# The last sum of a decoder layer: VectorE's adds for twelve of sixteen tiles become TensorE identity products

## Chip, cores, metric

The kernel runs on one core of a Trainium2 chip. The metric is device time in microseconds (us) of one execution, as the median of several. Lower is better.

## What is computed

One step of a decoder layer for 288 tokens (256 of a prompt, 32 samples) and a model width of 2048. Only the end of it matters here:

```python
hf = rms_norm(x, prm['norm_ffn_pre'][l])
f = jnp.square(jax.nn.relu(hf @ prm['ffn_w1'][l])) @ prm['ffn_w2'][l]
x = x + rms_norm(f, prm['norm_ffn_post'][l])

def rms_norm(x, g):
    y = xf * lax.rsqrt(jnp.mean(xf * xf, axis=-1, keepdims=True) + RMS_EPS)
    return (y * g).astype(x.dtype)
```

The last line is the output `o_y`: x plus the FFN output, scaled by one factor per feature (`g`) and one factor per token (the root).

## The kernel before

Activations lie with features on the 128 partitions and tokens along the free axis: x is `x_t`, 16 tiles of 128x288 (float32), in the memory named `arx`. The FFN output is `facc`, 16 tiles in `arm`. All big products run on TensorE as three single-pass products per weight tile (lines 429 to 431), for 1419 of the 1437 us. ScalarE and VectorE split the weights for them meanwhile (lines 393, 394).

The FFN runs in four blocks. In the last, the evacuation of each output tile m (lines 1830 to 1836) adds it into `facc`, squares it on ScalarE into `ssa` or `sqt`, multiplies `facc` by the feature's gain, and adds the squares into `ssa`. What follows the last product is a serial tail that no product covers:

- `sum_cols` (lines 409, 412): TensorE sums the squares over the partitions, first of `ssa`, then of `sqt[1]`, the last tile's squares.
- Square root on ScalarE (line 1848), reciprocal on VectorE (line 1849).
- `spread_cols` (line 418): TensorE spreads the 288 factors over all partitions, into a PSUM tile `ps`.
- For six groups of 1, 3, 4, 4, 3 and 1 tiles (`FIN`): VectorE multiplies `facc` by `ps` (line 1854) and adds it to `x_t` (line 1855); a store of the group follows, on SyncE's and ScalarE's queues in turn (line 1856).

A scheduler sets the order on each engine and adds the waits: every engine has a count that its instructions raise, and an instruction waits until another engine's count has reached a number. Operands are tracked by tile. The PSUM banks that the change uses are slices of one tile, handed out first in, first out:

```python
bt = psb.tile([128, 5, 512], F32, name="bt")
banks = Banks(bt, 5)
```

At the end all five are free.

Of the kernel before, what the change touches and what calls it, by code (L numbers as in the profile page):

```python
# [11 lines left out]
AF = mybir.ActivationFunctionType  # L12
# [5 lines left out]
NT = NP_ + NS  # L18
NB = 8
KT = D // 128  # L20
# [25 lines left out]
LEAD = 4  # L46
PRIO = {"gen_sample_scores": 0, "gen_sample_pv": 0, "gen_prompt_pv": 0.5}
BUDGET = 3.5
FIN = ((0, 1), (1, 3), (4, 4), (8, 4), (12, 3), (15, 1))
BUDO = 3.0  # L50
NSTR, LAG = 2, 3
GATE = 'TQ'
# [259 lines left out]
def build(tc, A, O):  # L312
    nc = tc.nc
    sy, dv, ac, po, pe = nc.sync, nc.vector, nc.scalar, nc.gpsimd, nc.tensor
    with ExitStack() as ctx:
# [12 lines left out]
        rc = cp.tile([128, 12], F32, name="rc")  # L328
        ssa = cp.tile([128, NT], F32, name="ssa")
        sqt = [cp.tile([128, NT], F32, name=f"sqt{i}") for i in range(2)]  # L330
# [6 lines left out]
        ident = ca[:, CA["ident"][0]:][:, :128]  # L337
        ones = ca[:, CA["ones"][0]:][:, :128]
# [9 lines left out]
        banks = Banks(bt, 5)  # L348
# [6 lines left out]
        facc = arm.rearrange("p (k t) -> p k t", k=KT)  # L355
# [48 lines left out]

        TOK = ((0, 0, 128), (1, 128, 128), (2, 160, 128))

        def sum_cols(ps, extra, srcs):

            pe.matmul(out=ps[:, 0:3], lhsT=ident, rhs=extra, start=True, stop=False)
            for j, src in enumerate(srcs):  # L410
                for i, lo, n in TOK:
                    pe.matmul(out=ps[:, i:i + 1], lhsT=src[:, lo:lo + n], rhs=ones[:, 0:1],  # L412
                              start=False, stop=(j == len(srcs) - 1 and i == 2))

        def spread_cols(ps, cols):

            for i, lo, n in ((0, 0, 128), (1, 128, 128), (2, 256, 32)):
                pe.matmul(out=ps[:, lo:lo + n], lhsT=cols[:, i:i + 1].to_broadcast([128, 128]),
                          rhs=ident[:, 128 - n:128], start=True, stop=True)

        def warm(n, lhsT, rhs):

            b = banks.get()
            for _ in range(n):
                pe.matmul(out=b[:, 0:128], lhsT=lhsT, rhs=rhs, start=True, stop=True)  # L425
            banks.put(b)
# [67 lines left out]
        def run_phase(seq, X, evac, budget):  # L494
            ps = None
            for m, h in seq:
                ci = advance()
                if h == 0:
                    ps = psm.tile([128, NT], F32, name="mm", tag="mm")
                for k in range(8):  # L500
                    if k == 6:
                        pump(budget)
                    xh, xl = X(h * 8 + k)
                    mm3(ps, whi[ci][:, k], wlo[ci][:, k], xh, xl, start=(h == 0 and k == 0), stop=(h == 1 and k == 7))
                del whi[ci], wlo[ci]
                st["done"] += 1
                if h == 1:
                    evac(m, ps)

        def tiles(lo, hi):  # L510
            return [(m, h) for m in range(lo, hi) for h in range(2)]
# [6 lines left out]
        x_t = arena.get(KT, NT, order=(0,))  # L518
# [47 lines left out]
        def gen_prenorm():  # L566
            yield 0
            b = banks.get()
            sum_cols(b, rc[:, 9:12], (ssa,))
            ac.activation(out=rc[:, 0:3], in_=b[:, 0:3], func=AF.Sqrt, scale=1.0 / D)  # L570
            dv.reciprocal(out=rc[:, 0:3], in_=rc[:, 0:3])
            spread_cols(b, rc[:, 0:3])
            ac.activation(out=rs_in, in_=b[:, :NT], func=AF.Copy)
            banks.put(b)
            arena.put(sq, x_t)
            S["pre"] = True
            yield 0.5
            sy.dma_start(out=cb, in_=A["c_b"])
            sy.dma_start(out=lora_in, in_=A["lora"][:, 0:512])
            sy.dma_start(out=lora_out, in_=A["lora"][:, 512:1024])  # L580
# [7 lines left out]
        def after(later, earlier):  # L588
            tc.add_manual_dep(later.ins, earlier.ins.name,
                              mybir.DependencyInfo(mybir.DependencyClass.NoSync, mybir.DependencyReason.DATA), reason="order")  # L590
# [1168 lines left out]
        x_t = X2[0]  # L1759
        ensure_split(st["use"] + 3)  # L1760
        ps = psm.tile([128, NT], F32, name="mm", tag="mm")
        sum_cols(ps, rc[:, 9:12], (ssa, sqt[1]))
        for m in range(KT - 2, KT):
            gain(m)
        warm(2, sqt[1][:, 0:128], ident)
        ac.activation(out=rc[:, 0:3], in_=ps[:, 0:3], func=AF.Sqrt, scale=1.0 / D)
        dv.reciprocal(out=rc[:, 0:3], in_=rc[:, 0:3])
        rs = banks.get()
        spread_cols(rs, rc[:, 0:3])
        warm(8, rc[:, 0:1].to_broadcast([128, 128]), ident)  # L1770

# [26 lines left out]
        def gen_ffnorm():  # L1798
            for _ in range(12):
                yield 0  # L1800
            for k in range(KT):
                sq = sqt[k % 2] if k else ssa
                ac.activation(out=sq, in_=x_t[:, k], func=AF.Square)
                if k:
                    dv.tensor_tensor(out=ssa, in0=ssa, in1=sq, op=ALU.add)
                if k % 2:
                    yield 0
            b, = yield from bk(1)
            sum_cols(b, rc[:, 9:12], (ssa,))
            dv.tensor_scalar(out=rc[:, 3:6], in0=b[:, 0:3], scalar1=1.0 / D, scalar2=None, op0=ALU.mult)  # L1810
            banks.put(b)
            yield 0.5
            dv.tensor_scalar(out=rc[:, 6:9], in0=rc[:, 3:6], scalar1=float(D * RMS_EPS), scalar2=None, op0=ALU.mult)
            dv.tensor_tensor(out=rc[:, 6:9], in0=rc[:, 6:9], in1=rc[:, 3:6], op=ALU.mult)
# [10 lines left out]
        def ev_w2(j):  # L1825
            def ev(m, ps):
                if j == 0:
                    ac.activation(out=facc[:, m], in_=ps, func=AF.Copy)
                else:
                    dv.tensor_tensor(out=facc[:, m], in0=ps, in1=facc[:, m], op=ALU.add)  # L1830
                if j == NBLK - 1:
                    sq = sqt[m % 2] if m else ssa
                    ac.activation(out=sq, in_=facc[:, m], func=AF.Square)
                    ac.activation(out=facc[:, m], in_=facc[:, m], func=AF.Copy, scale=pvc("fpost", m))
                    if 0 < m < 15:
                        dv.tensor_tensor(out=ssa, in0=ssa, in1=sq, op=ALU.add)
            return ev

        for j in range(NBLK):
# [3 lines left out]
            assert not gens  # L1843
            run_phase(tiles(0, 16), lambda k: (F["h"][:, k], F["l"][:, k]), ev_w2(j), 3.0)

        ps = psm.tile([128, NT], F32, name="mm", tag="mm")
        sum_cols(ps, rc[:, 6:9], (ssa, sqt[1]))
        ac.activation(out=rc[:, 0:3], in_=ps[:, 0:3], func=AF.Sqrt, scale=1.0 / D)
        dv.reciprocal(out=rc[:, 0:3], in_=rc[:, 0:3])
        ps = psm.tile([128, NT], F32, name="mm", tag="mm")  # L1850
        spread_cols(ps, rc[:, 0:3])
        for q, (lo, n) in enumerate(FIN):
            sl = slice(lo, lo + n)
            dv.tensor_tensor(out=facc[:, sl], in0=facc[:, sl], in1=ps.unsqueeze(1).to_broadcast([128, n, NT]), op=ALU.mult)  # L1854
            dv.tensor_tensor(out=x_t[:, sl], in0=x_t[:, sl], in1=facc[:, sl], op=ALU.add)  # L1855
            (ac if q % 2 else sy).dma_start(out=O["o_y"][:, sl], in_=x_t[:, sl])


def make(arrays):
    import concourse.bacc as bacc  # L1860

    nc = bacc.Bacc("TRN2", target_bir_lowering=False, num_devices=1)
    A = {n: nc.dram_tensor("in_" + n, a.shape, mybir.dt.from_np(a.dtype), kind="ExternalInput").ap() for n, a in arrays.items()}
    O = {n: nc.dram_tensor(n, s, F32, kind="ExternalOutput").ap() for n, s in OUTS.items()}
    with tile.TileContext(nc) as tc:
        build(tc, A, O)
    return nc
# [9 lines left out]
```

## Time and profile before

| | us |
|---|---|
| median of 3 runs | 1439.78 (1439.17 to 1441.64) |
| the profiled execution, its own time | 1438.48 |
| its span in the profile | 1436.7 |
| last big product ends | 1419.4 |
| VectorE's first multiply of the tail starts | 1422.65 |
| VectorE's last add ends | 1433.1 |

In a profile row, PE is TensorE's products, PEld its weight loads, DVE is VectorE, ACT is ScalarE, SPq the queue of SyncE. A float32 product stands as two records (x2), one of the big ones as one. A row gives start, duration, engine, line, operation, out<-in, shape, and in brackets how long the engine idled before it and what ended that.

### The profile page before, as it was taken

The page shows a single profiled execution, that of the slowest core. Times are in us where ns is not written, and L with a number is a line of the kernel's source. Part 1 is how long each engine was busy: PE and PEld are TensorE (multiplying, and loading weights), DVE is VectorE, ACT ScalarE, POOL GpSimd, SP SyncE. Part 2 cuts the span into 40 slices and gives each one's busy share as a digit, 9 for nine tenths or more (in the row PEclk, how much of TensorE's full clock was granted, in tenths as well). Part 3 has the DMA queues.
Part 4 walks back from the last instruction along what each step waited for, and adds up shares of the span by engine and source line. Part 5 has one row for each costly group of instructions (what it writes and reads, how often), then busy time and mean ns, then how long its engine had stood idle before and what let it go on. Part 6 is the DMA issues. An engine that isn't in the chain of part 4 may idle for free.

```text
span 1436.7 us, 27941 instructions
## 1 busy us (share of the span) xinstructions
PE 1399.8 (97%) x11730; PEld 1335.7 (93%) x11730; DVE 834.6 (58%) x1411; ACT 595.5 (41%) x857; POOL 57.4 (4%) x127
## 2 busy tenths in 40 slices
PE   8999999899999999999999999999999999999995
PEld 8899777787878999999999999999999999999995
DVE  7797557445797756794433455544455444555555
ACT  7433323332353534664433344333444333444442
POOL 2101012010101000000000000000000000000000
PEclk9999999999999999999999999999999999999998
DMA  8646678676859964354445444444444444444441
GB/s 291 178 150 213 222 270 265 234 283 219 283 182 379 320 219 163 117 160 165 162 165 172 164 162 165 171 163 164 169 166 163 164 171 164 162 166 169 165 164 79
DMA packets 86190, 276.62 MB, mean 193 GB/s; under 512 B 22400, under 2 KB 26032, under 8 KB 84016
## 3 DMA queue, kind: packets, MB, share of 16 engines
q1 hardware_dynamic: 75280, 212.23, 43.3%
q0 software_dynamic: 9920, 60.83, 11.7%
q8 instruction: 92, 1.51, 0.4%
q10 hardware_dynamic: 864, 1.77, 0.4%
q14 instruction: 34, 0.28, 0.1%
HBM read 267.97 MB, written 6.84 MB: 191 GB/s over the span
## 4 chain that ended last, share of the span: by engine, by line
PE 73%; DVE 1%; DMA 1%; ACT 1%; issue 0%; DVEq 0%
PE mm L429 23%; PE mm L430 23%; PE mm L431 23%; PE bt L1521 1%; DMA arx<-in_vc 1%; DVE arm L1854 0%; DVE arx L1855 0%; PE bt L1146 0%; PE bt L425 0%; ACT ring_h L393 0%; PE bt L1115 0%; DVE ring_l L394 0%; PE mm L412 0%; PE bt L429 0%; PE bt L1165 0%
## 5 line engine op out<-in xcount | busy, mean ns | idle before, releaser
L394 DVE TENSOR_TENSOR ring_l<-w,ring_h 128x1024 fp32r<-128x1024 f32 (+1 forms) x382 | 465.0, 1218 | 388.2 <-ACT ring_h L393 381.2
L393 ACT ACTIVATE ring_h<-w 128x1024 fp32r<-128x1024 f32 (+1 forms) x382 | 402.7, 1055 | 575.0 <-PE mm L430 510.4
L429 PE MATMUL mm<-hh,ring_h 128*128 128x288 f32 x1984 | 597.3, 301 | 5.2 <-ACT ring_h L393 3.3
L430 PE MATMUL mm<-hl,ring_h 128*128 128x288 f32 x1984 | 592.1, 299 | 0.0
L431 PE MATMUL mm<-hh,ring_l 128*128 128x288 f32 x1984 | 589.7, 298 | 0.2 <-DVE ring_l L394 0.2
L429 PEld LDWEIGHTS mm<-hh,ring_h 128*128 128x128 f32 x1984 | 373.4, 188 | 17.0 <-issue 8.5
L431 PEld LDWEIGHTS mm<-hh,ring_l 128*128 128x128 f32 x1984 | 374.6, 189 | 9.2 <-issue 6.3
L430 PEld LDWEIGHTS mm<-hl,ring_h 128*128 128x128 f32 x1984 | 374.3, 189 | 5.6 <-issue 3.3
L430 PE MATMUL mm<-fl,ring_h 128*128 128x288 f32 x1024 | 302.1, 295 | 0.0
L431 PE MATMUL mm<-fh,ring_l 128*128 128x288 f32 x1024 | 301.9, 295 | 0.0
L429 PE MATMUL mm<-fh,ring_h 128*128 128x288 f32 x1024 | 300.3, 293 | 0.0
L429 PEld LDWEIGHTS mm<-fh,ring_h 128*128 128x128 f32 x1024 | 192.5, 188 | 0.0
L430 PEld LDWEIGHTS mm<-fl,ring_h 128*128 128x128 f32 x1024 | 192.5, 188 | 0.0
L431 PEld LDWEIGHTS mm<-fh,ring_l 128*128 128x128 f32 x1024 | 192.4, 188 | 0.0
L1822 ACT ACTIVATE fh<-ft 128x288 fp32r<-128x288 f32 x64 | 28.3, 444 | 78.9 <-DVE ft L1821 78.9
L1830 DVE TENSOR_TENSOR arm<-mm,arm 128x288 f32<-128x288 f32 x48 | 22.0, 458 | 51.0 <-PE mm L431 51.0
L1823 DVE TENSOR_TENSOR fl<-ft,fh 128x288 fp32r<-128x288 f32 x64 | 29.2, 458 | 29.1 <-ACT fh L1822 29.1
L1821 DVE SCALAR_TENSOR_TENSOR ft<-mm,rt 128x288 f32<-128x288 f32 x63 | 28.2, 450 | 0.0
L1820 ACT ACTIVATE rt<-mm 128x288 f32<-128x288 f32 x63 | 24.9, 395 | 0.3 <-PE mm L431 0.3
L1438 PE MATMUL bt<-arm,ar 128*32 128x448 f32 x208 | 23.2, 546 | 1.3 <-DMA arm<-in_kc 1.0
L1729 DVE TENSOR_TENSOR ar<-mm,ar 128x288 f32<-128x288 f32 x32 | 14.5, 454 | 11.4 <-PE mm L431 11.4
L1406 POOL DMA_DIRECT2D arm<-in_kc x26 | 13.7, 528 | 98.3 <-PE bt L1438 90.8
(422 smaller groups left out, 893.1 us busy)
## 6 DMA issues: line engine op xcount, KB each, us to landing
w<-in_w SPq DMA_DIRECT2D x256, 512.0 KB
w<-in_w_in SPq DMA_DIRECT2D x91, 512.0 KB
arm<-in_kc POOLq DMA_DIRECT2D x26, 896.0 KB, 6.9
w<-in_w_out SPq DMA_DIRECT2D x32, 512.0 KB
arm<-in_vc POOLq DMA_DIRECT2D x9, 1024.0 KB, 7.1
ar<-in_vc POOLq DMA_DIRECT2D x7, 1024.0 KB, 7.7
arm<-in_vc POOLq DMA_DIRECT2D x9, 768.0 KB, 8.4
ar<-in_kc POOLq DMA_DIRECT2D x6, 896.0 KB, 7.6
```

The source lines that it names most:

```text
L393: ac.activation(out=h[:, lo:hi], in_=t[:, lo:hi], func=AF.Copy)
L394: dv.tensor_tensor(out=l[:, lo:hi], in0=t[:, lo:hi], in1=h[:, lo:hi].bitcast(F32), op=ALU.subtract)
L429: pe.matmul(out=ps, lhsT=h, rhs=xh, start=start, stop=False)
L430: pe.matmul(out=ps, lhsT=h, rhs=xl, start=False, stop=False)
L431: pe.matmul(out=ps, lhsT=l, rhs=xh, start=False, stop=stop)
L1438: pe.matmul(out=bh[32 * h:32 * h + 32, 0:448], lhsT=qz[:, h, b], rhs=t[:, h], start=(b == 0), stop=(b == NB - 1))
L1729: dv.tensor_tensor(out=macc(m), in0=ps, in1=macc(m), op=ALU.add)
L1820: ac.activation(out=r, in_=ps, func=AF.Relu)
L1821: dv.scalar_tensor_tensor(out=f, in0=ps, scalar=0.0, in1=r, op0=ALU.max, op1=ALU.mult)
L1822: ac.activation(out=fh[:, m], in_=f, func=AF.Copy)
L1823: dv.tensor_tensor(out=fl[:, m], in0=f, in1=fh[:, m].bitcast(F32), op=ALU.subtract)
L1830: dv.tensor_tensor(out=facc[:, m], in0=ps, in1=facc[:, m], op=ALU.add)
```

## The change

Of the sixteen last tiles, twelve (`FIN_PE`) no longer get VectorE's add. For each, TensorE opens a bank with identity times `x_t[:, k]` and, when VectorE has multiplied `facc[:, k]`, closes it with identity times `facc[:, k]`, which accumulates the sum; ScalarE copies the bank into `x_t` and a store takes two tiles. Tiles 12 to 15 stay with VectorE. All stores go through SyncE's queue. Four openings stand ahead of the chain (one inside `sum_cols`, two behind it, one behind `spread_cols`); opening k + 4 stands behind closing k. Multiplies take two tiles each, the last one four.

```diff
-FIN = ((0, 1), (1, 3), (4, 4), (8, 4), (12, 3), (15, 1))
+FIN_PE, FIN_DV = 12, ((12, 2), (14, 2))
...
+        def out_open(k, behind=None):
+            b = banks.get()
+            p = pe.matmul(out=b[:, :NT], lhsT=ident, rhs=x_t[:, k], start=True, stop=False)
+            if behind is not None:
+                after(p, behind)
+            return b
+
         ps = psm.tile([128, NT], F32, name="mm", tag="mm")
-        sum_cols(ps, rc[:, 6:9], (ssa, sqt[1]))
+        sum_cols(ps, rc[:, 6:9], (ssa,), last=False)
+        ob = [out_open(0)]
+        end = sum_cols(ps, None, (sqt[1],))
+        ob += [out_open(1, end), out_open(2, end)]
...
-        spread_cols(ps, rc[:, 0:3])
-        for q, (lo, n) in enumerate(FIN):
+        end = spread_cols(ps, rc[:, 0:3])
+        ob += [out_open(3, end)]
+
+        def times(lo, n):
             sl = slice(lo, lo + n)
             dv.tensor_tensor(out=facc[:, sl], in0=facc[:, sl], in1=ps.unsqueeze(1).to_broadcast([128, n, NT]), op=ALU.mult)
+
+        for lo in range(0, FIN_PE, 2):
+            times(lo, 2)
+            for k in (lo, lo + 1):
+                b = ob[k]
+                end = pe.matmul(out=b[:, :NT], lhsT=ident, rhs=facc[:, k], start=False, stop=True)
+                if k + 4 < FIN_PE:
+                    ob.append(out_open(k + 4, end))
+                ac.activation(out=x_t[:, k], in_=b[:, :NT], func=AF.Copy)
+                banks.put(b)
+            sy.dma_start(out=O["o_y"][:, lo:lo + 2], in_=x_t[:, lo:lo + 2])
+        times(FIN_PE, KT - FIN_PE)
+        for lo, n in FIN_DV:
+            sl = slice(lo, lo + n)
             dv.tensor_tensor(out=x_t[:, sl], in0=x_t[:, sl], in1=facc[:, sl], op=ALU.add)
-            (ac if q % 2 else sy).dma_start(out=O["o_y"][:, sl], in_=x_t[:, sl])
+            sy.dma_start(out=O["o_y"][:, sl], in_=x_t[:, sl])
```

Up to the column sums the order on every engine is that of before. Lines of the changed kernel stand 3 lower by then, or more. On TensorE, before, from the column sums to the end of the program (`ca` holds the identity and the ones, `rc` the small columns):

```order
L409 MATMUL mm<-rc,ca 128x3
L412 MATMUL mm<-ca,ssa 128x1 [waits DVE_49]
L412 MATMUL mm<-ca,ssa 128x1 x2
L412 MATMUL mm<-ca,sqt_77 128x1 [waits Activation_49]
L412 MATMUL mm<-ca,sqt_77 128x1 x2
L418 MATMUL mm<-ca,rc 128x128 [waits DVE_49]
```

Here TensorE has nothing to do between these steps. In the changed kernel, from the second half of the column sums to the third closing (line 1852 opens a bank, line 1876 closes it):

```order
L1852 MATMUL bt<-arx,ca 128x288 [waits DMAHW0_49]
L413 MATMUL mm<-ca,sqt_77 128x1 [waits Activation_49]
L413 MATMUL mm<-ca,sqt_77 128x1 x2
L1852 MATMUL bt<-arx,ca 128x288 x2
L420 MATMUL mm<-ca,rc 128x128 [waits DVE_49]
L420 MATMUL mm<-ca,rc 128x128
L420 MATMUL mm<-ca,rc 128x32
L1852 MATMUL bt<-arx,ca 128x288
L1876 MATMUL bt<-arm,ca 128x288 [waits DVE_49]
L1852 MATMUL bt<-arx,ca 128x288 [waits DMAHW4_49]
L1876 MATMUL bt<-arm,ca 128x288 [waits Activation_49]
L1852 MATMUL bt<-arx,ca 128x288
```

Three openings now stand ahead of `spread_cols`, and from tile 1 on every closing waits for ScalarE (Activation), though neither of its operands is written by ScalarE there; this goes on to tile 11. The numbers behind these waits in the built program: the square root leaves ScalarE's count at 824, and closing 1 waits for 825, which is the copy of tile 0. `spread_cols` leaves TensorE's count at 10477, opening 3, closing 0 and opening 4 make it 10478, 10479 and 10480, and the copy of tile 0 waits for 10480. Closing 1 and opening 5 raise it together to 10482, and the copy of tile 1 waits for that; so on to tile 11.

SyncE's queue, behind the last load, before:

```order
L1856 DMA o_y<-arx 128x288 [waits DVE_49]
L1856 DMA o_y<-arx 128x1152 [waits DVE_49]
L1856 DMA o_y<-arx 128x864 [waits DMAHW3_49,DVE_49]
```

And in the changed kernel (line 1881 stores a pair that ScalarE copied, line 1886 a pair that VectorE added):

```order
L1881 DMA o_y<-arx 128x576 [waits Activation_49]
L1886 DMA o_y<-arx 128x576 [waits DVE_49]
L1881 DMA o_y<-arx 128x576 [waits Activation_49]
L1886 DMA o_y<-arx 128x576 [waits DVE_49]
L1881 DMA o_y<-arx 128x576 [waits DMAHW3_49,Activation_49]
```

VectorE's two stores stand as second and fourth of eight, and the last one is that of tiles 10 and 11.

## Rows read from the trace of the kernel before

**Rows 1.** The page: the span, and busy time of each engine.

```profile
span 1436.7 us, 27941 instructions
PE 1399.8 (97%) x11730; PEld 1335.7 (93%) x11730; DVE 834.6 (58%) x1411; ACT 595.5 (41%) x857; POOL 57.4 (4%) x127
```

**Rows 2.** Timeline of the tail, from the last big product to the end.

```profile
1419.14 0.29 PE L431 MATMUL mm<-fh,ring_l 128*128 128x288 f32 x1
...
1419.41 0.81 PE L412 MATMUL mm<-ca,ssa 128*128 128x1 f32 x6
...
1420.46 0.83 PE L412 MATMUL mm<-ca,sqt 128*128 128x1 f32 x6 [0.24 <-ACT sqt L1833]
...
1421.76 0.85 PE L418 MATMUL mm<-ca,rc 128*128 128x128 f32 x6 [0.47 <-DVE rc L1849]
1422.65 1.42 DVE L1854 TENSOR_TENSOR arm<-arm,mm 128x288 f32<-128x288 f32 x2 [0.95 <-PE mm L418]
...
1425.33 2.61 DVE L1854 TENSOR_TENSOR arm<-arm,mm 128x1152 f32<-128x1152 f32 x2
...
1427.86 2.62 DVE L1855 TENSOR_TENSOR arx<-arx,arm 128x1152 f32<-128x1152 f32 x2
...
1431.72 1.42 DVE L1855 TENSOR_TENSOR arx<-arx,arm 128x864 f32<-128x864 f32 x2
```

**Rows 3.** Timeline: two float32 products back to back into two banks.

```profile
383.37 0.65 PE L1282 MATMUL bt<-arx 128*128 128x288 f32 x2
...
383.86 0.65 PE L1283 MATMUL bt<-arx 128*128 128x288 f32 x2
```

**Rows 4.** Timeline: product, copy, the next product behind the copy, and its copy.

```profile
402.29 0.65 PE L1172 MATMUL bt<-ar,ca 128*128 128x288 f32 x2
...
402.98 0.50 ACT L1173 ACTIVATE ar<-bt,eps 128x288 f32<-128x288 f32 x1 [0.90 <-PE bt L1172]
...
403.53 0.75 PE L1172 MATMUL bt<-ar,ca 128*128 128x288 f32 x2
...
404.32 0.50 ACT L1173 ACTIVATE ar<-bt,eps 128x288 f32<-128x288 f32 x1 [0.84 <-PE bt L1172]
...
404.88 0.54 PE L1521 MATMUL bt<-ar 128*32 128x128 f32 x12
```

**Rows 5.** Groups by line and shape: busy us, mean ns of one | idle before.

```profile
L1828 ACT ACTIVATE arm<-mm 128x288 f32<-128x288 f32 x16 | 6.3, 394 | 0.0
...
L1774 DVE TENSOR_TENSOR ar<-ar,bt 128x576 f32<-128x576 f32 x7 | 5.2, 748 | 1.0 <-PE bt L431 1.0
```

**Rows 6.** Stretches: length, busy of PE, PEld, DVE, ACT, POOL, granted clock, DMA.

```profile
232.20:235.60 3.40, 2.26 (x16) 1.91 (x14) 1.00 (x1) 1.06 (x1) 2.15 (x7) 1.00 1.04 327
235.60:239.00 3.40, 1.74 (x11) 1.63 (x12) 2.32 (x13) 0.00 (x0) 0.00 (x0) 1.00 0.97 338
...
590.60:594.00 3.40, 2.60 (x23) 2.51 (x22) 3.04 (x7) 2.89 (x6) 0.00 (x0) 1.00 0.54 190
594.00:597.40 3.40, 3.40 (x18) 3.40 (x18) 0.36 (x2) 0.28 (x2) 0.00 (x0) 0.50 0.46 159
597.40:600.80 3.40, 1.55 (x13) 1.36 (x13) 1.97 (x5) 0.75 (x2) 0.00 (x0) 1.00 0.00 0
600.80:604.20 3.40, 3.40 (x14) 3.10 (x15) 3.40 (x8) 2.17 (x6) 0.00 (x0) 0.51 0.00 0
1420.00:1423.40 3.40, 1.91 (x14) 1.62 (x14) 0.92 (x3) 1.12 (x3) 0.00 (x0) 1.00 0.00 0
1423.50:1426.90 3.40, 0.00 (x0) 0.00 (x0) 3.40 (x5) 0.00 (x0) 0.00 (x0) 0.50 0.31 119
```

**Rows 7.** Timeline: single-pass products at the lower clock.

```profile
602.18 0.44 PE L430 MATMUL mm<-hl,ring_h 128*128 128x288 f32 x1
602.42 0.44 PE L431 MATMUL mm<-hh,ring_l 128*128 128x288 f32 x1
602.66 0.44 PE L430 MATMUL mm<-hl,ring_h 128*128 128x288 f32 x1
```

More of the change, by code (lines that the diff above doesn't have):

```diff
@@ L405, in build, with sum_cols @@
         TOK = ((0, 0, 128), (1, 128, 128), (2, 160, 128))
-        def sum_cols(ps, extra, srcs):
-            pe.matmul(out=ps[:, 0:3], lhsT=ident, rhs=extra, start=True, stop=False)
+        def sum_cols(ps, extra, srcs, last=True):
+            if extra is not None:
+                pe.matmul(out=ps[:, 0:3], lhsT=ident, rhs=extra, start=True, stop=False)
             for j, src in enumerate(srcs):
                 for i, lo, n in TOK:
-                    pe.matmul(out=ps[:, i:i + 1], lhsT=src[:, lo:lo + n], rhs=ones[:, 0:1],
-                              start=False, stop=(j == len(srcs) - 1 and i == 2))
+                    p = pe.matmul(out=ps[:, i:i + 1], lhsT=src[:, lo:lo + n], rhs=ones[:, 0:1],
+                              start=False, stop=(last and j == len(srcs) - 1 and i == 2))
+            return p
         def spread_cols(ps, cols):
             for i, lo, n in ((0, 0, 128), (1, 128, 128), (2, 256, 32)):
-                pe.matmul(out=ps[:, lo:lo + n], lhsT=cols[:, i:i + 1].to_broadcast([128, 128]),
+                p = pe.matmul(out=ps[:, lo:lo + n], lhsT=cols[:, i:i + 1].to_broadcast([128, 128]),
                           rhs=ident[:, 128 - n:128], start=True, stop=True)
+            return p
         def warm(n, lhsT, rhs):
```

## Prediction

> **What bounds the kernel now.** I read the page first: TensorE is busy for 97% of a span of 1436.7 us [rows 1], so up to the last big product, which starts at 1419.14 [rows 2], the time is TensorE's. The change touches nothing before that: the order on every engine is the same up to the column sums. So I read the timeline of the tail. TensorE runs column sums and the spreading, with short waits between them, and from 1422.65 VectorE alone sets the end: twelve instructions, six multiplies and six adds, follow each other without a gap until 1433.14 (1431.72 + 1.42) [rows 2]. Two multiplies of 1152 columns start the two adds behind them 2.53 us later (1425.33 to 1427.86), which is 0.316 us for each tile of 288; 32 tiles, sixteen multiplied and sixteen added, make the 10.49 us. From there to the end of the span are 3.56 us: the last stores and the closing of the program. So the part at stake is 14.05 us long, 1422.65 to 1436.70.
>
> **VectorE's part.** Twelve adds go. Sixteen tiles of multiplies and four of adds stay: 20 x 0.316 = 6.3 us instead of 10.1, which would be worth nearly 4 us if VectorE still set the end. It doesn't, as the next parts show. Its work then lies beside TensorE's chain, and the stores of tiles 12 to 15 are ready about 6.5 us after the first multiply.
>
> **The price of one identity product.** These are full float32 products of 288 columns, and the trace has them: two back to back start 0.49 us apart (383.37 and 383.86) and one takes 0.65 us from its start to its result [rows 3]. One that has waited for another engine takes 0.75, since its weight load then lies on the path too [rows 4]. Twelve closings and twelve openings are 24 x 0.49 = 11.8 us of TensorE, more than the 10.5 us of VectorE's whole part before. Four of the openings stand ahead of the chain; 20 are in it.
>
> **The openings ahead of the chain.** Opening 0 lies between the two column sums, openings 1 and 2 ahead of the spreading, so three products, 1.45 us, go where TensorE idled 0.24 and 0.47 us [rows 2]. The bound above is 1.45 - 0.71 = 0.74 us of delay. Below, the queue of products can already take the next one while a result is still on its way: 0.65 - 0.49 = 0.16 at both places, and the 0.10 of weight load that the spreading no longer has behind a wait, which leaves some 0.35. I take 0.40, nearer to the lower end, since rows 3 show just this overlap. A gain is excluded: nothing is removed there. Opening 3 runs while VectorE multiplies the first pair.
>
> **The chain of waits.** This decides. The five banks are slices of one tile, and the waits in the built program are those of one tile: closing k + 1 waits for ScalarE's copy of tile k (count 825 for tile 1, where the square root leaves 824), and the copy of tile k waits for TensorE's count behind opening k + 4 (10480 for tile 0). So closing, opening, copy, next closing stand in a row; there is no overlap between ScalarE and TensorE, however many banks there are. What queues behind the waiting closing on TensorE is every later opening and closing; who waits for it is ScalarE's copy and the store of the pair.
>
> A round with an opening (k = 0 to 7): the second product starts 0.49 us behind the first and has its result 0.65 later [rows 3]; 0.10 come for the weight load behind the wait (0.75 against 0.65 [rows 3, 4]), and 0.04 until ScalarE starts (403.53 + 0.75 = 404.28, and 404.32 [rows 4]). The copy of a 128x288 PSUM tile by ScalarE takes 0.394 [rows 5]. From the end of a copy to the start of the product behind it are 0.05 us: 402.98 + 0.50 = 403.48, and the product starts at 403.53 [rows 4]. Sum 0.49 + 0.65 + 0.10 + 0.04 + 0.394 + 0.05 = 1.724 us. A round without one (k = 8 to 11): 404.32 - 403.53 = 0.79 from product to copy [rows 4], + 0.394 + 0.05 = 1.235. The trace has almost this round whole: 403.53 to 404.88 is 1.35 us, with a copy of 0.50 (it takes a root and a bias); with 0.394 it is 1.24 [rows 4]. I take the rounds from these rows, and as bounds 1.61 and 1.83 for the long ones (no weight load on the path; a copy of 0.50), 1.13 and 1.35 for the short ones.
>
> **The stores.** SyncE's queue holds the pair of 12 and 13 ahead of that of 2 and 3. It costs nothing: VectorE is done with both its adds about 6.5 us after its first multiply, and the copy of tile 3 ends after four rounds, later than that. The last store is that of tiles 10 and 11. For it and the closing of the program I take the 3.56 us of before [rows 2]; there the last stores were 432 and 144 KB, here it is 288 KB alone, so between 3.1 and 4.0.
>
> **The sum**, from VectorE's first multiply of before (1422.65): 0.40 for the openings ahead; 0.75 for the multiply of the first pair [rows 5] and 0.05 until closing 0 starts; 8 x 1.724 = 13.79; 4 x 1.235 = 4.94, less 0.05 since nothing follows the last copy; 3.56 to the end. That is 0.40 + 0.80 + 13.79 + 4.89 + 3.56 = 23.44 us in place of 14.05, so 9.4 us more. The profiled execution took 1438.48 us, 1.8 more than its span, and lies 1.3 under the median of 1439.78; its sum is 1447.9, and on the median it is 1439.78 + 9.39 = **1449.2 us**, 0.65% slower.
>
> **TensorE's clock.** Each round leaves TensorE idle for some 0.45 us. The granted clock fell from 2.4 to 1.2 GHz at 594.0, with TensorE busy for 2.60 of the 3.40 us before, most of it one-column sums and a pause, and at 600.8, with 1.55 of 3.40 busy; at 232.2 to 239.0 it stayed, with 2.26 and 1.74 of 3.40 [rows 6]. The long rounds have TensorE busy for 1.25 of 1.72 us with wide products, the short ones for 0.75 of 1.24, which lies between the row that kept the clock and those that lost it, nearer to the former. So I expect full clock for the long rounds, and a possible fall in the last 5 us. The Trainium skill (TensorE: Matmul & The Clock Gate, What's actually happening) has the clock fall back only after a spell of idleness; by that rule alone it would not fall here at all, and the sum stands as it is. The trace does not agree with it: at 594.0 TensorE had worked for 2.60 of the last 3.40 us.
>
> **Rivals.**
> *The clock falls in the chain.* At 1.2 GHz single-pass products start 0.24 us apart [rows 7], so a float32 product needs 0.96 in place of 0.49, and a long round some 2.8 us. The trace's lowered spells in which TensorE went on working were 594.0 to 597.4 and 600.8 to 604.2 [rows 6]; in 3.4 us 1.2 rounds pass and not 2, which costs 1.4 us: 1450.6 with one spell, 1452.0 with two. If the clock stayed low all along, 8 x 1.1 + 4 x 0.6 = 11 us: 1460. Against that stands that both of those spells ended while TensorE was busy. Chance 0.23, nearly all of it for one or two spells.
> *The copies wait for the closing alone.* Then the openings hide behind the copies and every round is 1.235: 18.68 becomes 14.77, and the time 1445.3. Against it speaks the count 10480. Chance 0.03.
> *Banks go their own ways, TensorE sets the pace (not slower).* If the waits were of single banks, closings and openings would follow each other: 20 x 0.49 = 9.8 us from closing 0, then 0.16 + 0.04 + 0.394 for the last copy, 10.4 in place of 18.68: 1440.9, no change. It decides from the point where a closing is released by VectorE and not by ScalarE. The Trainium skill (PSUM — Partial Sum Buffer, Terms) forbids two engines only the same bank at the same time, so by its rule the chip would allow this; no row here shows it, and the program's waits forbid it. Chance 0.04.
> *VectorE sets the end, as its shorter list would allow (faster).* 20 tiles x 0.316 = 6.3 us and 3.56: 1436.1. It needs what the last rival needs and an identity product under 0.32 us besides, against 0.49 [rows 3]. Chance 0.01.
>
> **How the numbers follow.** The forecast without a lowered clock has 0.69, the clock 0.23, the short rounds 0.03, free banks 0.04, VectorE 0.01. The bounds of the rounds (-1.3 to +1.4), the openings (-0.05 to +0.34) and the stores (-0.5 to +0.4) rarely fall on one side together: about 1.7 each way. The runs of before spread from 0.6 under to 1.9 over their median. With one or two lowered spells above, the range is 1446.7 to 1452.3. Within 0.2%, 2.9 us, is about what a measurement of this kernel can tell from no change. Faster 0.01, same 0.04, slower 0.95.
>
> **What would show it.** In the profile after: VectorE's first multiply near 1423.05; closings (line 1876) about 1.7 us apart for the first eight and 1.24 for the last four, each with idle time ended by ScalarE's copy (line 1879); copies of 0.39 us that each wait for line 1852 and not 1876; the last copy's end near 1442.5 and the span near 1446. The prediction is wrong if the closings come less than 1.2 us apart, if they wait for VectorE, or if a clock of 0.5 covers most of the chain.

## Result and profile after

The changed kernel took 1450.03 us (median of 4 runs, 1445.68 to 1452.59) against 1439.56 for the kernel before beside it (4 runs, 1439.17 to 1441.64). The ratio is 1.0071, with a 95% interval of 1.0056 to 1.0085: it is slower by 8 to 12 us, where 9.4 were forecast, and 1449.2 as the time. The profiled execution took 1445.68.

Two executions of one program differ by some us before the tail begins: the last big product starts at 1419.14 in the trace of before and anywhere from 1417.05 to 1423.91 in the kernels below, although the order on every engine is the same up to there; the differences come up ahead of 606 us. So the tails are compared directly: **tail** is the time from the start of the last big product to the end of the span. It is 17.56 us before (1419.14 to 1436.70, [rows 1, 2]) and 26.83 after (1417.05 to 1443.9 us), 9.27 more.

The page of the kernel after, its span and the busy time of each engine, which answers to [rows 1]:

```profile
span 1443.9 us, 28055 instructions
PE 1415.5 (98%) x11778; PEld 1344.0 (93%) x11778; DVE 831.0 (58%) x1408; ACT 600.1 (42%) x869; POOL 57.3 (4%) x127
```

By the page alone, VectorE has 3.6 us less to do, ScalarE 4.6 more, and TensorE 15.7 more; it is busier and the kernel slower. Where the time lies is read from the timeline of the tail after, which answers to [rows 2] (line 1870 multiplies, 1876 closes a bank, 1852 opens one, 1879 copies, 1885 adds on VectorE):

```profile
1417.05 0.29 PE L434 MATMUL mm<-fh,ring_l 128*128 128x288 f32 x1
...
1420.98 5.34 DVE L1870 TENSOR_TENSOR arm<-arm,mm 128x576 f32<-128x576 f32 x7 [1.29 <-PE mm L420]
...
1421.79 0.75 PE L1876 MATMUL bt<-arm,ca 128*128 128x288 f32 x2 [0.28 <-DVE arm L1870]
...
1422.38 0.65 PE L1852 MATMUL bt<-arx,ca 128*128 128x288 f32 x2
1423.07 0.41 ACT L1879 ACTIVATE arx<-bt 128x288 f32<-128x288 f32 x1 [3.58 <-PE bt L1852]
...
1423.53 0.75 PE L1876 MATMUL bt<-arm,ca 128*128 128x288 f32 x2 [0.50 <-ACT arx L1879]
...
1424.12 0.65 PE L1852 MATMUL bt<-arx,ca 128*128 128x288 f32 x2
1424.81 0.41 ACT L1879 ACTIVATE arx<-bt 128x288 f32<-128x288 f32 x1 [1.33 <-PE bt L1852]
...
1426.36 1.43 DVE L1885 TENSOR_TENSOR arx<-arx,arm 128x576 f32<-128x576 f32 x2
...
1436.95 0.75 PE L1876 MATMUL bt<-arm,ca 128*128 128x288 f32 x2 [0.50 <-ACT arx L1879]
...
1437.74 0.41 ACT L1879 ACTIVATE arx<-bt 128x288 f32<-128x288 f32 x1 [0.84 <-PE bt L1876]
...
1439.45 0.95 PE L1876 MATMUL bt<-arm,ca 128*128 128x288 f32 x2 [0.50 <-ACT arx L1879]
1440.43 0.41 ACT L1879 ACTIVATE arx<-bt 128x288 f32<-128x288 f32 x1 [1.04 <-PE bt L1876]
```

VectorE is done with everything at 1427.79 (1426.36 + 1.43), 10.74 us into the tail, against 14.00 before. But the last copy ends 13 us later, at 1440.84. In between one round follows another: closing 1 starts at 1423.53, its bank is copied from 1424.81, and the copy waits for line 1852, the opening of another bank, not for its own closing. The next closing waits for ScalarE's copy. The view of the waits in this stretch (engine and line that waits, <- the one waited for: us in all, times, longest) has it in three lines:

```profile
ACT arx L1879 <- PE bt L1852: 12.9, 8, 3.6
...
PE bt L1876 <- ACT arx L1879: 5.5, 11, 0.5
ACT arx L1879 <- PE bt L1876: 3.6, 4, 1.0
```

Eight copies wait for an opening, four for a closing, eleven closings for a copy: twelve rounds in a row, none beside another. Term by term, with the forecast in the last column:

| part of the tail after | us | forecast |
|---|---|---|
| first multiply later than before (3.94 against 3.51 into the tail) | 0.43 | 0.40 |
| first pair multiplied, until closing 0 | 0.81 | 0.80 |
| eight rounds with an opening, 1.738 each | 13.90 | 13.79 |
| four rounds without, to the end of the last copy | 5.15 | 4.89 |
| to the end of the span | 3.03 | 3.56 |
| sum | 23.32 | 23.44 |

### The profile page after: what moved, and what is told of

The parts are those of the page before. It is cut to its first block, busy times and chain, and to the rows that moved or that the text cites. A ratio compares the mean times of both kernels' runs of the same rounds, so it can differ in the third digit from the quotient of the medians.

```text
span 1443.9 us, 28055 instructions
## 1 busy us (share of the span) xinstructions
PE 1415.5 (98%) x11778; PEld 1344.0 (93%) x11778; DVE 831.0 (58%) x1408; ACT 600.1 (42%) x869; POOL 57.3 (4%) x127
## 4 chain that ended last, share of the span: by engine, by line
PE 73%; ACT 1%; DVE 1%; DMA 1%; issue 0%; DVEq 0%
PE mm L432 23%; PE mm L433 23%; PE mm L434 22%; PE bt L1524 1%; DMA arx<-in_vc 1%; PE bt L1876 1%; PE bt L1852 0%; ACT arx L1879 0%; PE bt L1149 0%; PE bt L428 0%; ACT ring_h L393 0%; PE bt L1118 0%; PE mm L413 0%; PE bt L432 0%; DVE ring_l L394 0%
```

## Experiments

All are edits of the changed kernel. Times of the kernel before were taken beside them on the same chip. Tails and ends come from one trace of each kernel.

| kernel | tail, us | VectorE ends | last copy ends | from the last engine's end to the end | median, us (runs) | before, us (runs) | ratio |
|---|---|---|---|---|---|---|---|
| before | 17.56 | 14.00 | none | 3.56 | | | |
| after | 26.83 | 10.74 | 23.80 | 3.03 | 1450.03 (4) | 1439.56 (4) | 1.0071 (1.0056 to 1.0085) |
| e1_own_banks | 18.20 | 10.74 | 15.16 | 3.04 | 1439.39 (10) | 1440.44 (23) | 1.0001 (0.9987 to 1.0016) |
| e2_no_openings | 24.76 | 10.74 | 21.73 | 3.04 | 1448.47 (6) | 1440.44 (23) | 1.0055 (1.0033 to 1.0077) |
| e3_half_copy | 25.20 | 10.74 | 22.16 | 3.03 | 1446.87 (6) | 1440.44 (23) | 1.0050 (1.0032 to 1.0067) |
| e4_four_on_pe | 17.18 | 13.08 | 9.70 | 4.09 | 1438.07 (10) | 1440.44 (23) | 0.9986 (0.9973 to 1.0000) |
| e5_spare_beside | 22.76 | 10.74 | 19.73 | 3.03 | 1445.85 (8) | 1438.84 (21) | 1.0046 (1.0032 to 1.0060) |
| e6_eight_own | 16.68 | 11.48 | 10.95 | 5.19 | 1438.50 (12) | 1438.84 (21) | 0.9992 (0.9980 to 1.0005) |
| e7_after_again | 27.39 | 10.74 | 24.35 | 3.04 | 1448.75 (6) | 1438.84 (21) | 1.0063 (1.0047 to 1.0078) |
| e8_eight_spread | 15.59 | 11.92 | 10.94 | 3.67 | 1438.67 (12) | 1440.63 (17) | 0.9989 (0.9977 to 1.0000) |

### e1: every bank a tile of its own

The theory is that the price lies in waits that the five slices share by being one tile. The rival is that it lies in the work, the products and copies themselves. The edit keeps all of the work:

```diff
-        psb = pool("psb", 1, space=PSUM)
+        pst = ExitStack()
+        psb = pst.enter_context(tc.tile_pool(name="psb", bufs=1, space=PSUM))
...
+        pst.close()
+        pso = pool("pso", 1, space=PSUM)
+        own = [pso.tile([128, 512], F32, name=f"ob{i}") for i in range(5)]
+        banks.b = list(own)
         ps = psm.tile([128, NT], F32, name="mm", tag="mm")
```

> The changed kernel with its five banks as five tiles of their own, so that closing k + 1 no longer waits for the copy of tile k; nothing else differs. The tail is counted from the start of the last big product to the end of the span: 17.6 us before, 26.8 with the change. Theory (the waits of one tile make the chain): the rounds go, TensorE's 20 products set the pace at 0.485 us each, 9.8 us from closing 0 to the last result instead of 18.5; tail 3.94 + 0.81 + 9.8 + 0.6 + 3.3 = 18.4 us, time near 1440.5. Rival (the path from TensorE to ScalarE and back is slow whatever the tiles are): closings still 1.74 us apart, tail 26.8, time near 1449.

Measured: a tail of 18.20 us where 18.4 were expected, 8.63 under that of after, and a time that can't be told from that of before. The timeline of this kernel (closings are line 1881, openings 1853, copies 1884):

```profile
1423.98 0.41 ACT L1884 ACTIVATE arx<-ob 128x288 f32<-128x288 f32 x1 [3.09 <-PE ob L1881]
...
1424.26 0.65 PE L1881 MATMUL ob<-arm,ca 128*128 128x288 f32 x2
...
1424.75 0.65 PE L1853 MATMUL ob<-arx,ca 128*128 128x288 f32 x2
1424.95 0.41 ACT L1884 ACTIVATE arx<-ob 128x288 f32<-128x288 f32 x1 [0.56 <-PE ob L1881]
...
1425.23 0.65 PE L1881 MATMUL ob<-arm,ca 128*128 128x288 f32 x2
...
1431.05 2.10 PE L1881 MATMUL ob<-arm,ca 128*128 128x288 f32 x8
...
1431.74 1.87 ACT L1884 ACTIVATE arx<-ob 128x288 f32<-128x288 f32 x4 [0.56 <-PE ob L1881]
```

Behind closing 0 no product waits any more: closings come 0.97 us apart (1424.26, 1425.23), two products of 0.485, and the last four 0.485 apart (2.10 us for four). Copies wait for their own closing, line 1881. The waits of this stretch have no line in which TensorE waits for ScalarE; these remain:

```profile
ACT arx L1884 <- PE ob L1881: 7.6, 9, 3.1
...
PE ob L1881 <- DVE arm L1875: 0.3, 1, 0.3
```

So 8.63 us of the 9.27 were the shared tile. What is left, 0.64, is TensorE's own pace: it works without a gap from closing 0 to the last closing, and the last copy ends 1.16 us later than VectorE did before, of which a shorter end behind it gives 0.52 back.

### e2 and e5: the openings in the chain, and the clock

e2 takes the eight openings out of the rounds (each bank from tile 4 on is closed without x, so x is missing in tiles 4 to 11):

```diff
-                end = pe.matmul(out=b[:, :NT], lhsT=ident, rhs=facc[:, k], start=False, stop=True)
+                end = pe.matmul(out=b[:, :NT], lhsT=ident, rhs=facc[:, k], start=(k >= 4), stop=True)
                 if k + 4 < FIN_PE:
-                    ob.append(out_open(k + 4, end))
+                    ob.append(banks.get())
```

> The changed kernel without the eight openings in the chain (4 to 11): the output of these tiles lacks x. Theory (a copy waits for the opening behind its closing): every long round becomes a short one, 8 x 0.485 = 3.9 us less; closings 1.25 us apart from the first on, tail 26.8 - 3.9 = 22.9 us, time near 1446. Rival (openings run beside the copies and cost nothing): tail 26.8, time unchanged.

The tail was 24.76 and not 22.9. All twelve rounds ought to have had 1.253 us, and the first eight had; then they grew to 1.53 and 1.83. The timeline of e2, one round early and one late:

```profile
1433.96 0.75 PE L1876 MATMUL bt<-arm,ca 128*128 128x288 f32 x2 [0.50 <-ACT arx L1879]
1434.75 0.41 ACT L1879 ACTIVATE arx<-bt 128x288 f32<-128x288 f32 x1 [0.84 <-PE bt L1876]
...
1436.74 1.33 PE L1876 MATMUL bt<-arm,ca 128*128 128x288 f32 x2 [0.50 <-ACT arx L1879]
1438.11 0.41 ACT L1879 ACTIVATE arx<-bt 128x288 f32<-128x288 f32 x1 [1.42 <-PE bt L1876]
```

ScalarE's copy is the same 0.41; the product takes 1.33 in place of 0.75. The view by stretches of e2 (start:end, length, busy time of PE, PEld, DVE, ACT and POOL with counts, granted clock, DMA share, GB/s):

```profile
1430.20:1435.20 5.00, 3.01 (x8) 1.19 (x8) 0.99 (x2) 1.65 (x4) 0.00 (x0) 1.00 0.60 236
1435.20:1440.20 5.00, 3.68 (x6) 1.29 (x6) 0.00 (x0) 1.09 (x3) 0.00 (x0) 0.54 0.30 118
```

The granted clock fell from 2.4 to 1.2 GHz near 1435.5, in the ninth closing, after eight rounds in which TensorE had worked 0.75 of every 1.25 us. So e2 left two things mixed. e5 is to part them: on top of the edit of e2, a product that nobody waits for, into a bank of another pool, fills the pause of each round:

```diff
+        spare = psm.tile([128, NT], F32, name="mm", tag="mm")
         for lo in range(0, FIN_PE, 2):
...
                 banks.put(b)
+                if k < 11:
+                    after(pe.matmul(out=spare, lhsT=ident, rhs=facc[:, k], start=True, stop=True), end)
```

> The run without openings in the chain again (the output of tiles 4 to 11 lacks x), and behind each closing but the last one more identity product into a bank of the other PSUM pool, which nothing reads and no copy waits for. In the run without it closings came 1.25 us apart until the clock fell, then 1.83, and the tail was 24.8 us. Theory (the copy's wait makes an opening cost, and the clock follows how much TensorE works): the spare product fits beside the copy, 0.59 + 0.485 = 1.08 of 1.25 us, so all closings are 1.25 apart, the granted clock stays at 1.0 to the last closing, and the tail is 24.8 - 2.1 = 22.7 us. Rivals: the spare product delays the next closing as an opening does (1.74 apart, tail 26.8); or the clock falls all the same (last four 1.8 apart or more, tail 24.8 or more).

The tail was 22.76, as expected. The timeline of e5 (closings line 1877, spare products 1883, copies 1880), and behind it its stretches:

```profile
1429.91 0.75 PE L1877 MATMUL bt<-arm,ca 128*128 128x288 f32 x2
...
1430.50 0.65 PE L1883 MATMUL mm<-arm,ca 128*128 128x288 f32 x2
1430.70 0.41 ACT L1880 ACTIVATE arx<-bt 128x288 f32<-128x288 f32 x1 [0.84 <-PE bt L1877]
...
1431.17 0.75 PE L1877 MATMUL bt<-arm,ca 128*128 128x288 f32 x2
```

```profile
1433.70:1438.70 5.00, 4.94 (x17) 2.70 (x17) 0.96 (x2) 1.65 (x4) 0.00 (x0) 1.00 0.60 236
1438.70:1443.70 5.00, 4.45 (x14) 2.31 (x14) 0.00 (x0) 1.64 (x4) 0.00 (x0) 1.00 0.30 118
```

Rounds of 1.253 us and a full clock throughout, although e5 has more products in the rounds (23) than the changed kernel (20). A product that no wait names is free in this chain; one of the same size that the copy's wait names costs 0.485. Against after the tail is 4.07 shorter: 8 x 0.485 = 3.88 for the openings, and 0.2 for the clock, which fell in after's last closing (0.95 in place of 0.75). Against e2 it is 2.00 shorter, which is what the clock cost there: everything else in the rounds is alike. That is one trace of each. All their executions are in line with it: the mean granted clock, as a share of 2.4 GHz, was 0.985 to 0.992 in the six of e2 and 0.991 to 0.995 in the eight of e5.

### e3: half a copy

If the copy lies in the row, halving it shortens every round by what it saves; if it runs beside TensorE's work, nothing changes. Half of each of the twelve tiles stays uncopied:

```diff
-                ac.activation(out=x_t[:, k], in_=b[:, :NT], func=AF.Copy)
+                ac.activation(out=x_t[:, k, :NT // 2], in_=b[:, :NT // 2], func=AF.Copy)
```

> The changed kernel with ScalarE's copies cut to 144 of 288 columns: the other half of the output of twelve tiles is x alone. By the rows of 288 and 512 columns (0.394 and about 0.595 us) a copy should take about 0.27 instead of 0.41 us. Theory (each copy is on the path): every round is 0.14 shorter, 12 x 0.14 = 1.6 us, long rounds 1.60 and short ones 1.11, tail 25.2 us. Rival (copies run beside TensorE's next products): tail 26.8.

The timeline of e3, the first copy and the closing behind it, twice:

```profile
1428.28 0.29 ACT L1879 ACTIVATE arx<-bt 128x144 f32<-128x144 f32 x1 [3.57 <-PE bt L1852]
...
1428.62 0.75 PE L1876 MATMUL bt<-arm,ca 128*128 128x288 f32 x2 [0.38 <-ACT arx L1879]
...
1429.90 0.29 ACT L1879 ACTIVATE arx<-bt 128x144 f32<-128x144 f32 x1 [1.33 <-PE bt L1852]
...
1430.24 0.75 PE L1876 MATMUL bt<-arm,ca 128*128 128x288 f32 x2 [0.38 <-ACT arx L1879]
```

A copy takes 0.29 in place of 0.41, a round 1.62 in place of 1.74, and the tail is 25.20, 1.63 shorter. The copy lies wholly in the row: what one round saves is what one copy saves. That the tail came out at the expected 25.2 is luck in part. A round saved 0.12 and not the expected 0.14, so twelve save 1.44; the other 0.19 are the last closing, in which the clock fell in after (0.95) and not in e3 (0.75). Half the columns save only 0.12 us, so 0.17 of 0.41, by this estimate, doesn't depend on them.

### e7: the changed kernel again

> The changed kernel once more, unaltered, for a second trace of the same program. Theory (the tail is fixed by the chain, and what differs between executions is the part before 431 us, where loads are waited for): tail 26.8 us within 0.4, closings 1.74 us apart for eight and 1.25 for four, ratio to before 1.0065. Rival (the chain itself varies, by the clock): the tail differs by 1 us or more from 26.8.

The first eleven closings came at the same times into the tail as in the first trace, to 0.03 us. The last one did not, as the timeline of e7 shows:

```profile
1440.71 0.92 PE L1876 MATMUL bt<-arm,ca 128*128 128x288 f32 x2 [0.50 <-ACT arx L1879]
...
1442.13 1.33 PE L1876 MATMUL bt<-arm,ca 128*128 128x288 f32 x2 [0.50 <-ACT arx L1879]
```

The clock fell 21.6 us into the tail here, one round earlier than in after (22.8), and the tail is 0.56 longer: that is all that differs. So the expected 0.4 was missed and the rival's 1 us not reached; the chain varies, but by the clock in its last rounds alone. The ratio of 1.0063 is 9.1 us of 1438.84, close to the difference of the tails; the 10.5 us between the medians of the first four runs each lie within the scatter of what runs ahead of the tail.

### e4: only four tiles on TensorE

With four tiles there is no opening inside a round, the chain ends early, and VectorE sets the end with 28 tiles of its work in place of 32:

```diff
-FIN_PE, FIN_DV = 12, ((12, 2), (14, 2))
+FIN_PE, FIN_DV = 4, ((4, 4), (8, 4), (12, 3), (15, 1))
...
-        times(FIN_PE, KT - FIN_PE)
         for lo, n in FIN_DV:
+            times(lo, n)
```

> Only four tiles on TensorE, all four opened ahead of the chain; VectorE adds the other twelve in groups of 4, 4, 3 and 1. Theory: four short rounds, 0.8 + 5.0 us, end long before VectorE does, which sets the end with 28 tiles of 0.316 instead of 32: 3.94 + 8.9 + 3.5 = 16.4 us of tail against 17.6 before, time near 1438.5, within 0.2% of before. Rival (products and copies beside it slow VectorE down, or the stores end later): tail 17.6 or more.

VectorE ended at 13.08 into the tail, 0.92 ahead of before, but the tail, 17.18 where 16.4 had been expected, is only 0.38 shorter. The rest was lost behind the last add: 4.09 us to the end in place of 3.56. There all 16 DMA engines are full, as the view by stretches of e4 shows (columns as above):

```profile
1430.00:1432.00 2.00, 0.00 (x0) 0.00 (x0) 2.00 (x4) 0.00 (x0) 0.00 (x0) 0.65 1.06 429
1432.00:1434.00 2.00, 0.00 (x0) 0.00 (x0) 0.29 (x1) 0.00 (x0) 0.00 (x0) 0.50 1.01 415
```

The 0.5 us were not in the sum, though the rival had named later stores. Whether the full DMA engines alone caused them, or also that SyncE's queue carries all the stores here where two queues shared them before, e4 doesn't part.

### e6 and e8: a version to beat both, and what its stores do to it

e6 takes the waits away as e1 does, gives eight tiles to TensorE and eight to VectorE, puts two of the openings behind the spreading, and sends the last store through ScalarE's queue:

```diff
-FIN_PE, FIN_DV = 12, ((12, 2), (14, 2))
+FIN_PE, FIN_DV = 8, ((8, 4, 4), (12, 4, 3), (15, 0, 1))
...
-        ob += [out_open(1, end), out_open(2, end)]
+        ob += [out_open(1, end)]
...
-        ob += [out_open(3, end)]
+        ob += [out_open(2, end), out_open(3, end)]
...
-        times(FIN_PE, KT - FIN_PE)
-        for lo, n in FIN_DV:
+        for lo, m, n in FIN_DV:
+            if m:
+                times(lo, m)
...
-            sy.dma_start(out=O["o_y"][:, sl], in_=x_t[:, sl])
+            (ac if lo == 15 else sy).dma_start(out=O["o_y"][:, sl], in_=x_t[:, sl])
```

> Five banks as tiles of their own, eight tiles on TensorE, eight on VectorE, one opening less ahead of the spreading, the last store one tile on ScalarE's queue. Theory (with banks of their own the engines overlap, and the longer list sets the end): VectorE has 24 tiles, 24 x 0.316 + 0.1 = 7.7 us, TensorE 12 products in the chain, 0.8 + 12 x 0.485 + 0.6 = 7.2 us; first multiply 3.6 us after the start of the last big product, tail 3.6 + 7.7 + 3.5 = 14.8 us against 17.6 before, 0.2% faster than before (1437.6 if before is 1440.4). Rival (reads of PSUM by VectorE and ScalarE and TensorE's writes hold each other up): VectorE's tiles take more than 0.35 us each, tail 16 us or more.

The engines kept to it: the last copy ends 10.95 and the last add 11.48 us into the tail, 2.5 us ahead of before. The tail was 16.68, and not 14.8: from the last add to the end are 5.19 us. That is the rival's number (16 or more) without its cause: VectorE took 0.33 us a tile (7.88 for 24). VectorE does all its multiplies first, for TensorE's tiles and for its own, so that its own stores all come at the end; the timeline of SyncE's queue in e6 and the view by stretches:

```profile
1430.37 0.43 SPq L1892 DMA_DIRECT2D o_y<-arx  x1
1430.97 0.34 SPq L1886 DMA_DIRECT2D o_y<-arx  x1
1431.40 1.00 SPq L1892 DMA_DIRECT2D o_y<-arx  x1
```

```profile
1428.00:1430.00 2.00, 2.00 (x10) 1.58 (x9) 2.00 (x2) 1.23 (x3) 0.00 (x0) 1.00 0.40 157
1430.00:1432.00 2.00, 0.49 (x3) 0.04 (x1) 1.48 (x3) 0.82 (x2) 0.00 (x0) 1.00 0.70 277
1432.00:1434.00 2.00, 0.00 (x0) 0.00 (x0) 0.00 (x0) 0.00 (x0) 0.00 (x0) 1.00 1.00 395
```

Stores of 576, 288, 432 and 144 KB, 1440 KB of the 2304 of the output, are issued between 1430.37 and 1432.4 (the last on ScalarE's queue, at 1431.51). The DMA engines are full from 1432 to 1434 at 395 GB/s with every other engine idle, while from 1428 to 1430 they were busy for 0.40.

e8 spreads them. VectorE's own tiles are multiplied and added in groups of three, three and two between the multiplies for TensorE, in a fixed order, and the last store, now of two tiles, is on ScalarE's queue again:

```diff
-FIN_PE, FIN_DV = 8, ((8, 4, 4), (12, 4, 3), (15, 0, 1))
+FIN_PE, FIN_DV = 8, {2: (8, 3), 6: (11, 3), 8: (14, 2)}
...
+            if lo in FIN_DV:
+                own_adds(*FIN_DV[lo])
+        own_adds(*FIN_DV[8])
```

> The run with eight tiles and banks of their own again, with VectorE's own eight tiles in three groups (3, 3, 2) put between its multiplies for TensorE, so that their stores leave earlier; the work is the same. In the run before it the engines were done 11.5 us after the start of the last big product, but the stores needed 5.2 us more, with all 16 DMA engines busy from 1432 to 1434. Theory (in that run the stores, all late, had become the end): VectorE again ends near 11.5, the stores need 3.6 us more, tail 15.1 us against 17.6 before and 16.7 in that run, 2.4 us under before. Rival (the end after the last store does not depend on when the others leave): tail 16.7 or more.

The stretches of e8:

```profile
1428.00:1430.00 2.00, 2.00 (x9) 1.33 (x7) 1.97 (x4) 1.29 (x4) 0.00 (x0) 1.00 0.81 324
1430.00:1432.00 2.00, 0.12 (x1) 0.00 (x0) 1.50 (x3) 0.49 (x2) 0.00 (x0) 1.00 0.81 325
```

VectorE ends 0.44 later than in e6 (11.92), with five changes between multiplying and adding in place of one, but the DMA engines are busy for 0.81 while the others still work, and from the last add to the end are 3.67 us. The tail is 15.59, where 15.1 had been expected, and 1.97 under that of before: the shortest of these traces. What gave the 1.52 us behind the last add isn't parted: the stores leave earlier and in other sizes, and no issue takes 1.00 us as one did in e6. The timed ratio is 0.9989 (0.9977 to 1.0000), at the edge of what can be told from no change, and 0.14% is what the tail would give. The timed ratios of e4, e6 and e8 overlap and don't rank them.

## Why the prediction was right

**The chain of waits** carried the forecast, and it is what the traces show: closings start 1.738 us apart where 1.724 were worked out, 1.253 where 1.235 were, each behind ScalarE's copy. The 0.014 to 0.018 us per round are in the main the copy: 0.410 in place of the 0.394 of [rows 5]. That the waits are the cause, and not the work, is shown by e1: the same work with a tile for each bank costs 0.64 us of tail in place of 9.27.

**The parts of a round** were sized from rows of other lines of the kernel, and each was tried by itself: an opening is worth 0.485 (e5 against after), the copy counts in full (e3), and the weight load behind a wait is there (a closing takes 0.75 after a wait, and its weight load starts with it; in e1 it takes 0.65, and its weight load starts 0.24 ahead; as in [rows 3, 4]).

**The stores** were the one term outside its bounds: 3.03 against 3.56 taken and 3.1 as the least. Where one store of 288 KB, of a pair that ScalarE copied, is the last, the end lies 3.03 to 3.04 us behind that copy, in all six kernels of which this holds (after, e1, e2, e3, e5, e7). The 3.56 of before are those of the last two stores, 576 KB together, and the bound was set too near to them; that the size makes the difference was not tried by itself. That the sum came within 0.12 of the measured 23.32 is luck in part: the stores were 0.53 too large, and the other terms together 0.41 too small, 0.26 of it in the four short rounds, of which 0.2 were the clock.

**VectorE's list** takes 6.80 us from first multiply to last add, not 6.3: sixteen tiles in twos and one four cost more per tile than the 0.316 of fours [rows 2]. The same goes for the list of before: 32 x 0.316 is 10.1, and not the 10.49 that the prediction says it makes. The list lies beside the chain, so nothing came of it.

**The clock.** The forecast was full clock in the long rounds and a possible fall in the last 5 us. So it was: in after it fell in the last closing, in e7 one round earlier, in the 13.9 us of long rounds never. The view by stretches of after, the long rounds and then the short ones:

```profile
1421.80:1435.70 13.90, 9.90 (x33) 5.42 (x33) 5.95 (x8) 3.28 (x8) 0.00 (x0) 1.00 0.27 106
1435.70:1440.90 5.20, 3.20 (x8) 1.18 (x8) 0.00 (x0) 1.64 (x4) 0.00 (x0) 0.90 0.29 113
```

The rows that the prediction compared did not carry this forecast: by its busy share a long round (1.25 of 1.72 us) lies nearer to the stretch that lost the clock with 2.60 of 3.40 than to the one that kept it with 2.26, and no order by busy share parts the rows that kept it from those that lost it [rows 6]. So the right call here owes something to luck. What the experiments add: in e2, with nothing but short rounds, the clock fell in the ninth closing and cost 2.00 us, and a round at 1.2 GHz took 0.57 us more, where the prediction had 0.6. With an opening in each round (after) or a spare product (e5) it did not fall there. The Trainium skill (TensorE: Matmul & The Clock Gate, What's actually happening) has the clock fall back after idleness. e2 does not agree with that as it stands: no pause of TensorE between its closings was longer than 0.50 us.

**The rivals.** That the copies wait for their closings alone is out by the waits of line 1879 on line 1852. That the banks go their own ways is out for the changed kernel, but it is what e1 makes true, and its price was right: 10.4 us from closing 0 to the end of the last copy were worked out, and e1 has 10.41 (15.16 less 4.75). The Trainium skill (PSUM — Partial Sum Buffer, Terms) keeps two engines only from the same bank at the same time. e1 agrees: there ScalarE copies out of one bank in 0.41 us while TensorE's products go into others at their full pace of 0.485.

**What the prediction did not see** is that the price was one of bookkeeping that could be removed. It named this as a rival's condition and no more. And what e1 then yields is nothing: with twelve tiles its last copy ends 15.16 us into the tail, where VectorE was done at 14.00 before. With eight tiles both engines end close together (10.95 and 11.48 us in e6), which they do in neither kernel.

## What to carry to other kernels

Where work is handed between two engines through slices of one buffer, read from the waits whose work each handover names: if a copy waits for a product into another slice, the buffers are one for the scheduler, and any number of them gives no overlap; a tile for each is the remedy. Before moving work off the engine that sets the end, sum it on the new one: the split at which both end together is what shortened the tail here (e6, e8), not the largest that can be moved. And look at the last stores: in e6 2.5 us of faster engines became 0.9 us of tail, with more than half of the output issued within 2 us around VectorE's last add.

## What was not expected of the hardware

- The granted clock fell to 1.2 GHz while TensorE worked 0.75 of every 1.25 us with wide products (e2, near 1435.5), and stayed at 2.4 where a product that nobody needs filled the pause (e5). That useless product was worth 2.00 us of tail.
- In stretches of 2 us in which stores alone kept the DMA engines full, they moved 395 to 429 GB/s (a share of 0.98 and 406 GB/s before, 1.06 and 429 in e4, 1.00 and 395 in e6). The end of these kernels lay 3.56 (before), 4.09 (e4) and 5.19 us (e6) behind the last add, against 3.03 to 3.04 behind the last copy with one last store of 288 KB. One store's issue on SyncE's queue took 1.00 us in e6 beside 0.33 to 0.43 for the others there. What lengthened it was not tried.

The line of before for the second point, 1430 to 1432, in the view by stretches:

```profile
1430.00:1432.00 2.00, 0.00 (x0) 0.00 (x0) 2.00 (x4) 0.00 (x0) 0.00 (x0) 0.50 0.98 406
```
